# Decay rows fetched by DMA through a ring of four with a GpSimd mask, and rotation tables built first as outer products, in a hybrid SSM and attention trunk

## The chip, the cores and the metric

One Trainium2 chip, of which the kernel uses one core. The time is the device time of one execution in microseconds (us), the median over several runs. Engines are named as the profile names them: PE (TensorE; PEld is its weight load), DVE (VectorE), ACT (ScalarE), POOL (GpSimd) and SP (SyncE, which only issues DMAs here).

## The reference

The input is 2048 rows of 1024 float32 values. One layer is computed, and a final RMSNorm:

```python
h = rmsnorm(x, mix_norm_w)
proj = h @ w_in                          # columns: u | z | xbc | dt
y_s5  = s5_mixer(u, ...)                 # 16 groups of 16 channels, 64 complex states each
y_ssd = ssd_mixer(z, xbc, dt, ...)       # Mamba-2: 12 heads of 64, state 128, chunks of 128 rows
x = x + concat(y_s5, y_ssd) @ w_out
x = x + cross_attention(rmsnorm(x), rmsnorm(mem))      # 4 heads, 256 memory rows
x = x + conv_ffn(rmsnorm(x))                           # gated, causal convolution of width 3
out = rmsnorm(x)
```

Two pieces of it matter here. In `ssd_mixer` every head and chunk has a decay matrix:

```python
a_cs = cumsum(dt * a)                                  # 128 values per chunk and head
seg  = a_cs[l] - a_cs[s]
lmat = exp(where(l >= s, seg, -inf))                   # 128 x 128 per chunk and head
y_diag = (C B^T * lmat) @ (x * dt)
```

In `s5_mixer` a state rotates by a fixed complex angle with every row; the kernel works in strides of eight rows, and for that needs tables of the cosine and sine of 256 multiples of the stride's angle, for 16 groups x 64 states (1024 x 256 values each).

## The kernel before

The kernel runs its stages one after the other: the mixer (input projection, S5 preparation and SSD), the S5 stage and the output projection, the attention, the FFN. An fp32 product is made as three matmuls (`mm3`): both factors are split into a high and a low part, for a weight by ACT (L98) and DVE (L99). A loaded weight of 128x512 becomes 12 matmuls so; it is called a weight half below, as `proj` uses two of them for one projection of 512 rows.

The mixer walks over four blocks of 512 rows. A block has 22 projections, 44 weight halves. After each half `k.step()` advances two lists of generators by one yield: the foreground list has the SSD work of the block (`ssd`, in two passes `pr` of six heads), the background list has what can be done at any time: `norm1_rest` (the first norm of x's row tiles t4 to t15, whose first four, t0 to t3, are done at the start), `s5_setup`, sums of squares, preparation of the memory. This fixes the program's order; a scheduler of the tile framework then orders the instructions of each engine by its own estimates, and each engine takes its list in that order. Tiles come from pools with a fixed number of buffers (`t` has 28 of 128x512, `u` has 14 of 128x384); an instruction that wants a buffer waits until the last reader of its former content is done. `k.load` puts the weight loads on SP's queue (L111).

A norm of a row tile goes over three engines: ACT squares and sums (`ss`, L136), DVE scales (L130), POOL takes the power -0.5 (L131), DVE multiplies the row by it (L139).

`dtprep` makes `acs`, the cumulative sums of a block (128 rows x 4 chunks x 12 heads), packs a high and a low part of it into `pk`, and transposes it into `rows` (L382 to L391). `ssd` gets the decay matrices L (128 x 4 chunks x 6 heads x 128) from it: for each head one matmul that spreads the head's row over all partitions (`sel` x `rows`, L409), one that adds the mask's -1e30 (`idr` x `mask`, L410), and four exps on ACT (L412) that subtract the row's own sum (`nacs`). DVE multiplies with L at L425 and L441.

`s5_setup` computes the S5 coefficients: sines and cosines, the loads of the matrices b and c (L654), the products that go to DRAM as `cct`, `ww`, and, last, the tables. For these, `Er` and `Ei` hold the sines and cosines of the angle times powers of two, and POOL doubles a table of one column up to 256 columns, eight times for two groups each (L742 to L758), with buffers of the `t` and `u` pools, and stores it to `tabd`.

Of the kernel before, what the change touches and what calls it, by code (L numbers as in the profile page):

```python
# [173 lines left out]
class MixerIn:  # L174


    def __init__(self, k, cx, a, dram, T):
# [8 lines left out]
        x3 = flat(self.lp.tile([P, 4, 6, P], F32, tag="L", name="L").rearrange("p c h l -> p c (h l)"))  # L186
# [43 lines left out]
        sl = c([44, 12], "sl")  # L230
        V.tensor_tensor(sl, k.ident[0:44, 0:12], k.ident[0:44, 32:44], op=ALU.add)
        self.sel = []
        for i in range(3):
            s = k.t(F32R, p=44)
            V.tensor_copy(s.rearrange("p (a b) -> p a b", a=4), bcol(sl[:, 4 * i:4 * i + 4], P))
            self.sel += [s[:, q * 128:q * 128 + 128] for q in range(4)]
# [106 lines left out]
    def dtprep(self, hs, b):  # L343
# [28 lines left out]
        dt, da, acs, hr, nacs, E, cd = sm("dt"), sm("da"), sm("acs"), sm("hr", F32R), sm("nacs"), sm("E"), sm("cd")  # L372
# [9 lines left out]
        pk = self.pk[b % 2]  # L382
        V.tensor_copy(hr, acs)
        V.tensor_copy(pk[:, :, 0:12], r4(hr.bitcast(F32)))
        V.tensor_tensor(pk[:, :, 32:44], r4(acs), r4(hr.bitcast(F32)), op=ALU.subtract)
        yield
        pr = k.ps()
        for c in range(4):
            TE.transpose(pr[0:44, c * 128:c * 128 + 128], pk[:, c, :], k.ident)
        rows = k.t(F32R, p=44)  # L390
        S.activation(rows, pr[0:44, :], AF.Copy)  # L391
# [5 lines left out]
        self.dd = dict(dt=dt, rows=rows, nacs=nacs, E=E, cd=cd)  # L397
        yield

    def ssd(self, b, pr, dd, xs, Bs, Cs, zs, sqacc):  # L400
# [4 lines left out]
        L = self.lp.tile([P, 4, 6, P], F32, tag="L", name="L")  # L405
        for hh in range(6):
            h = pr * 6 + hh
            p = k.ps()
            TE.matmul(p, self.sel[h], dd["rows"], start=True, stop=False)  # L409
            TE.matmul(p, self.idr, self.mask.rearrange("p (a b) -> p a b", a=1).to_broadcast([P, 4, P]), start=False, stop=True)  # L410
# [7 lines left out]
        def stage_in(c):  # L418
            cs = slice(c * 128, c * 128 + 128)
            px = k.ps()  # L420
            for i in range(3):
                TE.transpose(px[:, i * 128:i * 128 + 128], xs[i][:, cs], k.ident)
            xdt, xdd = self.u(), self.u()
            V.tensor_tensor(r6(xdt), r6(px[:, 0:384]), v6(dd["dt"], c), op=ALU.mult)
            V.tensor_tensor(r6(xdd), r6(xdt), L[:, c, :, 127:128].to_broadcast([P, 6, 64]), op=ALU.mult)  # L425
            pB = k.ps()
            for i in range(2):
                TE.transpose(pB[:, i * 128:i * 128 + 128], Bs[i][:, cs], k.ident)
            Bt = self.u(256)
            S.activation(Bt, pB[:, 0:256], AF.Copy)  # L430
            st[c] = [xdt, xdd, Bt]

        def stage_cb(c):
            cs = slice(c * 128, c * 128 + 128)
            pc = k.ps()
            for i in range(2):
                TE.matmul(pc[:, i * 128:i * 128 + 128], Bs[i][:, cs], Cs[i][:, cs], start=True, stop=True)
            M = [self.u() for _ in range(2)]
            for i in range(2):
                m3 = M[i].rearrange("p (h l) -> p h l", h=3)  # L440
                V.tensor_tensor(m3, L[:, c, i * 3:i * 3 + 3, :], pc[:, i * 128:i * 128 + 128].rearrange("p (h l) -> p h l", h=1).to_broadcast([P, 3, P]), op=ALU.mult)  # L441
            st[c].append(M)
# [113 lines left out]
def s5_setup(k, a, d, up, NJ):  # L556
# [54 lines left out]
    yield  # L611

# [109 lines left out]
    r8 = d["r8"]  # L722
    V.tensor_tensor(r8, mag, mag, op=ALU.mult)
    V.tensor_tensor(r8, r8, r8, op=ALU.mult)
    V.tensor_tensor(r8, r8, r8, op=ALU.mult)
# [4 lines left out]
    for q in range(nst + 2):  # L730
        e, f = Er[:, q, :], Ei[:, q, :]
        V.tensor_tensor(t1, e, f, op=ALU.mult)
        V.tensor_scalar(Ei[:, q + 1, :], t1, 2.0, None, op0=ALU.mult)
        V.tensor_tensor(t1, e, e, op=ALU.mult)
        V.tensor_tensor(u1, f, f, op=ALU.mult)
        V.tensor_tensor(Er[:, q + 1, :], t1, u1, op=ALU.subtract)
    yield
    for gq in range(8):
        gs = slice(gq * 2, gq * 2 + 2)
        tc_, ts_ = k.t(), k.t()  # L740
        c3, s3 = (v.rearrange("p (g j) -> p g j", g=2) for v in (tc_, ts_))
        G.memset(c3[:, :, 0:1], 1.0)  # L742
        G.memset(s3[:, :, 0:1], 0.0)
        for q in range(nst):
            m = 1 << q
            tt = up(256).rearrange("p (g j) -> p g j", g=2)[:, :, 0:m]
            er, ei = bcol(Er[:, 3 + q, gs], m), bcol(Ei[:, 3 + q, gs], m)
            co, so, ci, si = c3[:, :, m:2 * m], s3[:, :, m:2 * m], c3[:, :, 0:m], s3[:, :, 0:m]
            G.tensor_tensor(co, ci, er, op=ALU.mult)
            G.tensor_tensor(tt, si, ei, op=ALU.mult)  # L750
            G.tensor_tensor(co, co, tt, op=ALU.subtract)
            G.tensor_tensor(so, ci, ei, op=ALU.mult)
            G.tensor_tensor(tt, si, er, op=ALU.mult)
            G.tensor_tensor(so, so, tt, op=ALU.add)
            if q >= 4:
                yield
        for h, v in ((0, c3), (1, s3)):
            G.dma_start(out=d["tab"][gs, :, h, :].rearrange("g p n -> p g n"), in_=v)  # L758
        yield
# [751 lines left out]
def trunk(tc, a, out, T):  # L1511
    with ExitStack() as cx:
# [6 lines left out]
                 tab=D([16, P, 2, NJ], "tabd"), ww=D([16, P, 256], "wwd"), cct=D([16, P, 384], "cctd"), Gt=D([4, 4, P, 512], "Gtd"), VWt=D([4, 4, P, 512], "VWtd"), p=D([T, 1024], "pd"), act=D([T // 128, P, 22, 128], "actd"),  # L1519
# [64 lines left out]
```

## Time and profile before

| | |
|---|---|
| median of three runs | 2716.18 us (2715.41 to 2720.42) |
| the profiled execution | 2718.37 us, its span 2716.6 us |
| mean granted clock of TensorE | 0.995 |
| busy: PE, DVE, ACT, POOL | 98%, 78%, 49%, 18% of the span |
| instructions | 38,961 |
| DMA | 455.6 MB, 168 GB/s on average |

The profile is of one execution. A group line has the source line, the engine, the operation and `out<-in` by the program's names, with `xcount`, busy time and the mean of one in ns; a window line has the length of the window and then, for each engine, the busy time and the number of instructions, the granted clock, the DMA share and GB/s. The tables are what POOL does between 600 and 760 us:

```profile
POOL 0000000059912110110311222211111110000000
```

This is POOL's busy share in 40 slices of 68 us, in tenths.

### The profile page before, as it was taken

The numbers are of one execution on the slowest core, as the hardware profiler recorded it, in microseconds if no ns is written. First come the engines' busy times: TensorE is split into PE (matmuls) and PEld (weight loads), VectorE is DVE, ScalarE is ACT, GpSimd is POOL, SyncE is SP. The second block draws the span as 40 slices with busy tenths as digits, with TensorE's granted clock in tenths as the row PEclk, the third lists the DMA queues.
The fourth block names the chain that finished last, engine by engine and source line by source line (L and its number), as shares of the span: only waits on it lengthen the run. The fifth ranks groups of instructions, "written<-read, shape, count | busy, mean of one in ns | idle before, by whom it ended". The sixth has DMA issues, their size and how long they took to land. (4 is left out here: it accounts for less than half of the span.)

```text
span 2716.6 us, 38961 instructions
## 1 busy us (share of the span) xinstructions
PE 2656.7 (98%) x12744; PEld 2200.2 (81%) x12744; DVE 2119.4 (78%) x4032; ACT 1322.1 (49%) x2661; POOL 484.6 (18%) x991
## 2 busy tenths in 40 slices
PE   8999999999899999999999999999999999999997
PEld 6878878788788788887888888888888888788876
DVE  8687888887777655788789788889878787677776
ACT  5565455544445413788645555345434344333233
POOL 0000000059912110110311222211111110000000
PEclk9999999999999999999999999999999999999999
DMA  6453343332378865536664333425222228887886
GB/s 196 137 160 126 94 133 108 115 100 88 109 238 270 307 235 178 175 127 237 239 220 151 113 120 122 140 83 182 86 87 85 78 63 270 273 293 239 261 268 201
DMA packets 238851, 455.57 MB, mean 168 GB/s; under 512 B 29432, under 2 KB 71416, under 8 KB 238648
## 3 DMA queue, kind: packets, MB, share of 16 engines
q1 hardware_dynamic: 182312, 341.38, 38.4%
q0 software_dynamic: 27728, 92.82, 10.5%
q10 hardware_dynamic: 28608, 18.88, 2.2%
q8 instruction: 101, 1.65, 0.3%
q14 instruction: 102, 0.84, 0.1%
HBM read 338.09 MB, written 114.29 MB: 167 GB/s over the span
## 5 line engine op out<-in xcount | busy, mean ns | idle before, releaser
L123 PE MATMUL ps<-H,W 128*128 128x512 f32 x952 | 370.7, 389 | 0.0
L125 PE MATMUL ps<-H,W 128*128 128x512 f32 x952 | 370.4, 389 | 0.0
L124 PE MATMUL ps<-H,W 128*128 128x512 f32 x952 | 370.3, 389 | 0.0
L123 PE MATMUL ps<-h,w 128*128 128x512 f32 (+1 forms) x736 | 298.6, 406 | 2.4 <-DVE h L102 1.5
L125 PE MATMUL ps<-h,w 128*128 128x512 f32 (+1 forms) x736 | 285.2, 388 | 0.0
L124 PE MATMUL ps<-h,w 128*128 128x512 f32 (+1 forms) x736 | 284.6, 387 | 0.1
L123 PE MATMUL ps<-Q,A 128*128 128x512 f32 x704 | 275.9, 392 | 1.7 <-ACT A L98 0.6
L125 PE MATMUL ps<-Q,A 128*128 128x512 f32 x704 | 274.4, 390 | 0.0
L124 PE MATMUL ps<-Q,A 128*128 128x512 f32 x704 | 274.0, 389 | 0.0
L98 ACT ACTIVATE w<-r 128x512 fp32r<-128x512 f32 x224 | 140.9, 633 | 254.2 <-PE ps L124 190.4
L98 ACT ACTIVATE W<-S 128x512 fp32r<-128x512 f32 x191 | 118.9, 630 | 282.0 <-DVE S L1337 144.8
L125 PEld LDWEIGHTS ps<-H,W 128*128 128x128 f32 x952 | 178.7, 188 | 37.1
L124 PEld LDWEIGHTS ps<-H,W 128*128 128x128 f32 x952 | 178.7, 188 | 37.0
L123 PEld LDWEIGHTS ps<-H,W 128*128 128x128 f32 x952 | 178.7, 188 | 36.9
L99 DVE TENSOR_TENSOR w<-r,w 128x512 fp32r<-128x512 f32 x224 | 158.0, 707 | 45.4 <-ACT w L98 42.3
L125 PEld LDWEIGHTS ps<-h,w 128*128 128x128 f32 x736 | 138.6, 188 | 29.6
L123 PEld LDWEIGHTS ps<-h,w 128*128 128x128 f32 x736 | 139.0, 189 | 28.2 <-DVE h L102 1.7
L124 PEld LDWEIGHTS ps<-h,w 128*128 128x128 f32 x736 | 139.2, 189 | 25.6 <-DVE h L102 1.4
L123 PEld LDWEIGHTS ps<-Q,A 128*128 128x128 f32 x704 | 132.2, 188 | 29.3 <-ACT A L98 0.9
L125 PEld LDWEIGHTS ps<-Q,A 128*128 128x128 f32 x704 | 132.2, 188 | 28.4 <-DVE A L99 0.8
L124 PEld LDWEIGHTS ps<-Q,A 128*128 128x128 f32 x704 | 132.2, 188 | 26.7
L98 ACT ACTIVATE A<-F 128x512 fp32r<-128x512 f32 (+1 forms) x146 | 89.1, 631 | 124.6 <-PE ps L124 71.2
(485 smaller groups left out, 6344.3 us busy)
## 6 DMA issues: line engine op xcount, KB each, us to landing
A<-actd SPq DMA_DIRECT2D x192, 256.0 KB, 3.9
r<-in_w_in SPq DMA_DIRECT2D x176, 256.0 KB, 2.9
R<-in_w_up SPq DMA_DIRECT2D x176, 256.0 KB, 2.9
R<-in_w_down SPq DMA_DIRECT2D x132, 256.0 KB, 4.2
actd<-U POOLq DMA_DIRECT2D x88, 256.0 KB, 3.3
A<-actd SPq DMA_DIRECT2D x96, 192.0 KB, 3.7
R<-h3Cd SPq DMA_DIRECT2D x56, 256.0 KB, 3.5
X<-in_x SPq DMA_DIRECT2D x16, 512.0 KB, 6.3
```

Source lines behind the costliest of these rows:

```text
L98: self.S.activation(hi, src, AF.Copy)
L99: self.V.tensor_tensor(lo, src, hi.bitcast(F32), op=ALU.subtract)
L123: self.TE.matmul(out, lh, rh, start=first and i == 0, stop=False)
L124: self.TE.matmul(out, lh, rl, start=False, stop=False)
L125: self.TE.matmul(out, ll, rh, start=False, stop=last and i == n - 1)
```

## The change

The decay matrices: `acs` is transposed once per block (48 rows of 128), copied to SBUF and stored to DRAM (`acsd`). `fetch_L` reads the six rows of one chunk and one pass back, broadcast to all 128 partitions (128x768), into one of four slots of `Ls`, and lets POOL write -1e30 above the diagonal with an `affine_select`. Both the DMA and the mask are on POOL's list. ACT's exps run in place in the slot. The first two chunks of a block are asked for in `dtprep`, the third at the start of `ssd`, each other one three chunks ahead of its use.

The tables: they are built right after the sines and cosines, ahead of the rest of `s5_setup`. A number j = 16 a + b: two small tables of 16 columns each for the 16 groups (`fc`, `fs` for a and for b) are doubled up in 48 products, and each of the 16 groups is then an outer product of the two by the angle sum formulas, six products of 128x256 and one store. The small tables live in the buffers in which the matrices b and c come later (tags 5b1, 5b2, 5Ca, 5Cb). The `u` and `t` pools are not used for the tables any more; `t` has 25 buffers.

```diff
@@ setup
-        mk = k.t(n=P)
-        V.tensor_scalar(mk, self.tri, 1e30, -1e30, op0=ALU.mult, op1=ALU.add)
-        self.mask = c([P, P], "mask", F32R)
-        V.tensor_copy(self.mask, mk)
-        self.idr = c([P, P], "idr", F32R)
-        V.tensor_copy(self.idr, k.ident)
...
@@ dtprep
-        pk = self.pk[b % 2]
-        V.tensor_copy(hr, acs)
-        V.tensor_copy(pk[:, :, 0:12], r4(hr.bitcast(F32)))
-        V.tensor_tensor(pk[:, :, 32:44], r4(acs), r4(hr.bitcast(F32)), op=ALU.subtract)
         yield
         pr = k.ps()
-        for c in range(4):
-            TE.transpose(pr[0:44, c * 128:c * 128 + 128], pk[:, c, :], k.ident)
-        rows = k.t(F32R, p=44)
-        S.activation(rows, pr[0:44, :], AF.Copy)
+        TE.transpose(pr[0:48, 0:P], acs, k.ident)
+        rows = self.sp.tile([48, P], F32, tag="rows", name="rows")
+        V.tensor_copy(rows, pr[0:48, 0:P])
+        k.G.dma_start(out=self.d["acs"][b].rearrange("c h l -> (c h) l"), in_=rows)
+        for c in range(2):
+            self.fetch_L(b, 0, c)
...
+    def fetch_L(self, b, pr, c):
+        L = self.Ls[:, self.nL % 4]
+        self.nL += 1
+        self.k.G.dma_start(out=L.rearrange("p h l -> p (h l)"), in_=flat(self.d["acs"][b, c:c + 1, pr * 6:pr * 6 + 6, :]).partition_broadcast(P))
+        self.k.G.affine_select(out=L, in_=L, pattern=[[0, 6], [1, P]], compare_op=ALU.is_ge, fill=-1e30, base=0, channel_multiplier=-1)
+        self.L[b, pr, c] = L
@@ ssd
-        L = self.lp.tile([P, 4, 6, P], F32, tag="L", name="L")
-        for hh in range(6):
-            h = pr * 6 + hh
-            p = k.ps()
-            TE.matmul(p, self.sel[h], dd["rows"], start=True, stop=False)
-            TE.matmul(p, self.idr, self.mask.rearrange("p (a b) -> p a b", a=1).to_broadcast([P, 4, P]), start=False, stop=True)
-            for c in range(4):
-                S.activation(L[:, c, hh, :], p[:, c * 128:c * 128 + 128], AF.Exp, bias=dd["nacs"][:, c * 12 + h:c * 12 + h + 1])
-            if hh % 2 or pr and b == self.NB - 1:
-                yield
+        Ls = {}
+        def decay(c):
+            L = Ls[c] = self.L.pop((b, pr, c))
+            for hh in range(6):
+                h = c * 12 + pr * 6 + hh
+                S.activation(L[:, hh, :], L[:, hh, :], AF.Exp, bias=dd["nacs"][:, h:h + 1])
+        if pr == 0:
+            self.fetch_L(b, 0, 2)
+        decay(0)
+        yield
...
         for c in range(4):
             stage_cb(c)
+            n = pr * 4 + c + 3
+            if n < 8:
+                self.fetch_L(b, n // 4, n % 4)
+            if c < 3:
+                decay(c + 1)
             yield
@@ s5_setup, after the sines and cosines
+    Er, Ei = (sp.tile([P, nst + 3, 16], F32, tag=n, name=n) for n in ("Er", "Ei"))
...
+    tw = sp.tile([P, 16, 8], F32, tag="tw", name="tw")
+    few = []
+    for n, q0 in (("B", 3), ("A", 7)):
+        fc, fs = (sp.tile([P, 16, 16], F32, tag="5" + x, name="f" + x) for x in (("b1", "b2") if n == "B" else ("Ca", "Cb")))
...
+        for q in range(4 if n == "B" else nst - 4):
...
+            G.tensor_tensor(co, ci, er, op=ALU.mult)
+            G.tensor_tensor(t, si, ei, op=ALU.mult)
+            G.tensor_tensor(co, co, t, op=ALU.subtract)
+            G.tensor_tensor(so, ci, ei, op=ALU.mult)
+            G.tensor_tensor(t, si, er, op=ALU.mult)
+            G.tensor_tensor(so, so, t, op=ALU.add)
+            yield
+        few.append((fc, fs))
+    (cb, sb), (ca, sa) = few
+    for g in range(16):
+        tab = sp.tile([P, 2, na, 16], F32, tag="tab", name="tab", bufs=2)
+        wk = sp.tile([P, 16, 16], F32, tag="5Ba", name="wk")[:, 0:na]
...
+        G.tensor_tensor(tab[:, 0], a_(ca), b_(cb), op=ALU.mult)
+        G.tensor_tensor(wk, a_(sa), b_(sb), op=ALU.mult)
+        G.tensor_tensor(tab[:, 0], tab[:, 0], wk, op=ALU.subtract)
+        yield
+        G.tensor_tensor(tab[:, 1], a_(sa), b_(cb), op=ALU.mult)
+        G.tensor_tensor(wk, a_(ca), b_(sb), op=ALU.mult)
+        G.tensor_tensor(tab[:, 1], tab[:, 1], wk, op=ALU.add)
+        G.dma_start(out=d["tab"][g], in_=tab.rearrange("p h a b -> p h (a b)"))
+        yield
@@ s5_setup, at its end: the doubling over 256 columns goes
-    for gq in range(8):
-        tc_, ts_ = k.t(), k.t()
...
-            tt = up(256).rearrange("p (g j) -> p g j", g=2)[:, :, 0:m]
...
-            G.tensor_tensor(co, ci, er, op=ALU.mult)
...
-        for h, v in ((0, c3), (1, s3)):
-            G.dma_start(out=d["tab"][gs, :, h, :].rearrange("g p n -> p g n"), in_=v)
@@
-            k.open(c1, 3, r=8, w=8, h=16, t=28)
+            k.open(c1, 3, r=8, w=8, h=16, t=25)
```

Three places show how the instructions stand now. The first is POOL in block 0. Before, its list has after the setup only the eighteen `ss` powers of the row tiles, and then the stores of S5 products:

```order
L220 AFFINE_SELECT tri<-tri 128x128
L229 AFFINE_SELECT last<-last 128x128
L131 TENSOR_TENSOR ss<-ss,m_71 128x1 x18
L131 TENSOR_TENSOR rs<-rs,m_71 128x4
L680 DMA cctd<-t 128x4x128
L699 MEMSET t 128x512
```

After, this is a piece around the power of tile t7 (`tab`, `wk`, `fCa`, `fb` are the new tables and their parts; `m_71` is the constant -0.5):

```order
L388 AFFINE_SELECT L<-L 128x768
L656 TENSOR_TENSOR tab<-tab,wk 128x256
L654 TENSOR_TENSOR tab<-fCa,fb_3017 128x256
L659 TENSOR_TENSOR wk<-fCa,fb_3018 128x256
L658 TENSOR_TENSOR tab<-fCb,fb_3017 128x256
L660 TENSOR_TENSOR tab<-tab,wk 128x256
L661 DMA tabd<-tab 128x512
L655 TENSOR_TENSOR wk<-fCb,fb_3018 128x256
L131 TENSOR_TENSOR ss<-ss,m_71 128x1
L656 TENSOR_TENSOR tab<-tab,wk 128x256
L659 TENSOR_TENSOR wk<-fCa,fb_3018 128x256
```

The power of t7 stands behind the small products, 21 of the large ones, and the first four fetches with their masks; those of t8 and t9 stand 38 and 28 large products further down.

The second is DVE at the same place, the scaling of t7 with the weight halves around it. Before:

```order
L99 TENSOR_TENSOR w<-r,w 128x512
L322 COPY t<-halo 128x3
L130 TENSOR_SCALAR ss<-ss 128x1
L139 TENSOR_SCALAR raw<-raw,ss 128x1024
L331 SCALAR_TENSOR_TENSOR t<-t 128x512
```

After:

```order
L99 TENSOR_TENSOR w<-r,w 128x512
L130 TENSOR_SCALAR ss<-ss 128x1
L139 TENSOR_SCALAR raw<-raw,ss 128x1024
L309 COPY halo<-t 128x3
L313 SCALAR_TENSOR_TENSOR t<-t,cw 128x512
```

The scaling stood behind the 19th weight half and stands behind the 20th; what has moved is POOL's side of the pair.

The third is SP, where the loads of the matrices b and c stand. Before they come after 14 weight loads, and their buffers are empty:

```order
L111 DMA r<-in_w_in 128x512
L654 DMA b_2997<-in_s_b 128x256
L654 DMA b_2998<-in_s_b 128x256
L654 DMA Ca<-in_s_c 128x256
L654 DMA Cb<-in_s_c 128x256
L111 DMA r<-in_w_in 128x512
```

After they come behind 37 weight loads, and go into the buffers that the small tables were read from:

```order
L705 DMA b_4924<-in_s_b 128x256
L705 DMA Cb<-in_s_c 128x256
L111 DMA r<-in_w_in 128x512
L705 DMA b_4925<-in_s_b 128x256
L705 DMA Ca<-in_s_c 128x256
L111 DMA r<-in_w_in 128x512 x3
```

So each of the four waits for POOL's last reader of that buffer, with the weight loads behind it on SP.

More of the change, by code (lines that the diff above doesn't have):

```diff
@@ L185, in __init__ @@
         cp = self.cp
-        x3 = flat(self.lp.tile([P, 4, 6, P], F32, tag="L", name="L").rearrange("p c h l -> p c (h l)"))
+        self.Ls, self.nL, self.L = self.lp.tile([P, 4, 6, P], F32, name="L"), 0, {}
+        x3 = flat(self.Ls.rearrange("p c h l -> p c (h l)"))
         self.x0 = [x3[:, 0:1024], x3[:, 1024:2048], x3[:, 2048:3072], k.raw()]
@@ L229, in __init__ @@
         G.affine_select(out=self.last, in_=self.last, pattern=[[0, P]], compare_op=ALU.is_ge, fill=0.0, base=-127, channel_multiplier=1)
[L230 to L236, printed above, removed]
         wdr = c([P, 96], "wdr")
@@ L246, in __init__ @@
         V.memset(self.halo, 0.0)
-        self.pk = [c([P, 4, 44], f"pk{i}") for i in range(2)]
-        for q in self.pk:
-            V.memset(q, 0.0)
         self.prev = [self.u() for i in range(2)]
@@ L396, in dtprep @@
         S.activation(cd, pc[:, 0:48], AF.Exp)
-        self.dd = dict(dt=dt, rows=rows, nacs=nacs, E=E, cd=cd)
+        self.dd = dict(dt=dt, nacs=nacs, E=E, cd=cd)
         yield
+    def fetch_L(self, b, pr, c):
[4 more added lines that the diff above has]
+        self.L[b, pr, c] = L
     def ssd(self, b, pr, dd, xs, Bs, Cs, zs, sqacc):
@@ L424, in stage_in @@
             V.tensor_tensor(r6(xdt), r6(px[:, 0:384]), v6(dd["dt"], c), op=ALU.mult)
-            V.tensor_tensor(r6(xdd), r6(xdt), L[:, c, :, 127:128].to_broadcast([P, 6, 64]), op=ALU.mult)
+            V.tensor_tensor(r6(xdd), r6(xdt), Ls[c][:, :, 127:128].to_broadcast([P, 6, 64]), op=ALU.mult)
             pB = k.ps()
@@ L611, in s5_setup @@
     yield
+    r8 = d["r8"]
+    V.tensor_tensor(r8, mag, mag, op=ALU.mult)
+    V.tensor_tensor(r8, r8, r8, op=ALU.mult)
+    V.tensor_tensor(r8, r8, r8, op=ALU.mult)
+    nst = NJ.bit_length() - 1
+    Er, Ei = (sp.tile([P, nst + 3, 16], F32, tag=n, name=n) for n in ("Er", "Ei"))
+    V.tensor_copy(Er[:, 0, :], cs)
+    V.tensor_copy(Ei[:, 0, :], sn)
+    for q in range(nst + 2):
+        e, f = Er[:, q, :], Ei[:, q, :]
+        V.tensor_tensor(t1, e, f, op=ALU.mult)
+        V.tensor_scalar(Ei[:, q + 1, :], t1, 2.0, None, op0=ALU.mult)
+        V.tensor_tensor(t1, e, e, op=ALU.mult)
+        V.tensor_tensor(u1, f, f, op=ALU.mult)
+        V.tensor_tensor(Er[:, q + 1, :], t1, u1, op=ALU.subtract)
+        if q % 4 == 3:
+            yield
@@ L1518, in trunk @@
                  yT=D([T // 128, P, 8, 128], "yTd"), x1=D([T, 1024], "x1d"), x2=D([T, 1024], "x2d"), h3C=D([T // 1024, 7, 4, P, 512], "h3Cd"),
-                 tab=D([16, P, 2, NJ], "tabd"), ww=D([16, P, 256], "wwd"), cct=D([16, P, 384], "cctd"), Gt=D([4, 4, P, 512], "Gtd"), VWt=D([4, 4, P, 512], "VWtd"), p=D([T, 1024], "pd"), act=D([T // 128, P, 22, 128], "actd"),
+                 tab=D([16, P, 2, NJ], "tabd"), ww=D([16, P, 256], "wwd"), cct=D([16, P, 384], "cctd"), Gt=D([4, 4, P, 512], "Gtd"), VWt=D([4, 4, P, 512], "VWtd"), p=D([T, 1024], "pd"), acs=D([T // 512, 4, 12, P], "acsd"), act=D([T // 128, P, 22, 128], "actd"),
                  rs=k.cp.tile([P, T // 128], F32, name="rs"), r8=k.cp.tile([P, 16], F32, name="r8"))
         with ExitStack() as c1:
-            k.open(c1, 3, r=8, w=8, h=16, t=28)
+            k.open(c1, 3, r=8, w=8, h=16, t=25)
             mem = Memory(k, a, d)
```

46 lines of the change are left out of this document (12 added, 34 removed).

## The prediction

> **What bounds the kernel now.** I read the engine totals first, then windows of a quiet and of a disturbed stretch, then the waits of the latter. The totals, and the two windows (length, then busy time and instructions of PE, PEld, DVE, ACT and POOL, granted clock, DMA share, GB/s):
>
> ```profile
> PE 2656.7 (98%) x12744; PEld 2200.2 (81%) x12744; DVE 2119.4 (78%) x4032; ACT 1322.1 (49%) x2661; POOL 484.6 (18%) x991
> 100.00:200.00 100.00, 99.35 (x511) 80.22 (x511) 74.56 (x167) 58.98 (x128) 3.19 (x5) 1.00 0.48 148
> 600.00:760.00 160.00, 146.21 (x798) 123.96 (x797) 119.81 (x233) 74.03 (x162) 125.06 (x313) 0.96 0.32 102
> ```
>
> PE is the bound: 98% busy over the span, 99.35 us of 100 in block 0. A matmul that goes is therefore time won at its start-to-start distance, as long as DVE and ACT, which prepare PE's weights, keep ahead. The exception is 600 to 760 us, where POOL, almost idle elsewhere, is busy for 125 us building the rotation tables. PE idles there for 13.8 us at a mean clock of 0.96, another 6.4 us worth: 20 us together. The largest waits of that stretch are these (engine, what waits, for what: total us, times, longest):
>
> ```profile
> DVE u L452 <- POOL t L754: 6.5, 2, 3.9
> DVE u L424 <- POOL t L754: 6.0, 3, 3.5
> DVE u L441 <- POOL t L754: 3.5, 2, 2.2
> ```
>
> DVE waits for the `u` buffers that POOL's table code also takes from. That coupling goes with the change.
>
> **The products removed.** One stretch of PE's timeline (start, duration, instruction) and the groups by form (count, busy, mean ns):
>
> ```profile
> 94.54 0.49 PE L409 MATMUL ps<-t 44*128 44x512 f32 x1
> 94.96 0.49 PE L410 MATMUL ps<-mask,idr 128*128 128x512 f32 x1
> 95.39 0.49 PE L409 MATMUL ps<-t 44*128 44x512 f32 x1
> L410 PE MATMUL ps<-mask,idr 128*128 128x512 f32 x48 | 23.9, 497 | 0.0
> L409 PE MATMUL ps<-t 44*128 44x512 f32 x48 | 23.8, 495 | 0.0
> L389 PE MATMUL ps<-ident,pk 128*44 128x128 f32 x16 | 2.4, 272 | 0.0
> ```
>
> They start 0.42 us apart (94.54, 94.96, 95.39), so 96 of them hold PE for 40.3 us; 12 of the 16 transposes go too, at an estimated 0.1 us of pitch each (a quarter of the 512-wide row). Of the 96, 12 belong to the first half of block 0 and lie in front of the delay worked out next, which swallows them. The other 84 and 9 transposes are worth 84 × 0.42 + 0.9 = **-36.1 us**, all on the path. With them go the packing of `pk` and `hr` on DVE, one ACT copy a block and the setup of `sel`, `mask` and `idr`: none of it was the last thing PE waited for; I cost it at 0, covered by the weights in flight, at most -2.
>
> **The tables moved to the front.** This is the largest term. POOL's stream now has, in block 0: the sums of squares `ss` (L131) of the first x tiles, 48 small products, then 16 groups of six 128x256 products and a DMA, with the first four decay fetches, their masks, and the `ss` of tiles t7, t8 and t9 between them. An engine takes its instructions in order, which the 25.88 us of the first row below show: a POOL DMA waited for ACT with ready products behind it. Durations from the old tables and nearby rows:
>
> ```profile
> 543.02 0.77 POOL L680 DMA_DIRECT2D wwd<-t  x1 [25.88 <-ACT t L719]
> 643.77 0.73 POOL L749 TENSOR_TENSOR t<-t,Er 128x16 f32<-128x16 f32 x1
> 652.97 0.61 POOL L749 TENSOR_TENSOR t<-t,Er 128x256 f32<-128x256 f32 x1
> L749 POOL TENSOR_TENSOR t<-t,Er 128x256 f32<-128x256 f32 x8 | 5.3, 667 | 0.0
> L750 POOL TENSOR_TENSOR u<-t,Ei 128x256 f32<-128x256 f32 x8 | 6.3, 791 | 0.0
> L751 POOL TENSOR_TENSOR t<-t,u 128x256 f32<-128x256 f32 x8 | 7.1, 892 | 0.6
> L752 POOL TENSOR_TENSOR t<-t,Ei 128x256 f32<-128x256 f32 x8 | 4.9, 612 | 0.0
> L753 POOL TENSOR_TENSOR u<-t,Er 128x256 f32<-128x256 f32 x8 | 6.2, 778 | 0.6
> L754 POOL TENSOR_TENSOR t<-t,u 128x256 f32<-128x256 f32 x8 | 6.9, 864 | 0.2
> 637.20 0.79 POOL L758 DMA_DIRECT2D tabd<-t  x1
> 639.07 0.73 POOL L758 DMA_DIRECT2D tabd<-t  x1 [0.22 <-POOL t L743]
> L1460 POOL DMA_DIRECT2D F<-in_final_norm_w x1 | 0.6, 558 | 0.0
> L699 POOL MEMSET t<- 128x512 f32 x4 | 2.2, 549 | 0.0
> L220 POOL TENSOR_SCALAR_AFFINE_SELECT tri<-tri 128x128 f32<-128x128 f32 x1 | 0.3, 293 | 0.0
> t<-cctd POOLq DMA_DIRECT2D x16, 192.0 KB, 5.0
> ```
>
> From 643.77 to 652.97 the old code ran the four doublings of 16, 32, 64 and 128 elements, 24 products: 9.2 us. The new code runs two such builds, 18.4 us. A group of the new tables is the sum of the six means, 4.60, and 0.73 for the DMA: 5.3 us (bounds: six at 0.61 and 0.73, 4.4; six at 0.892 and 0.79, 6.1). The mask over 128x768 has no row: the 128x128 one took 0.293, six of those would be 1.76, and a fill of 512 elements scaled to 768 gives 0.82; I take 1.3, the middle, as both neighbours are far. Four fetches and the store of the rows are five issues at 0.56, the four masks 5.2, and the first mask waits for its rows to land, 5.0 less three issues: 3.3. Together 11.3 us. Where POOL stands against DVE, in the trace of before:
>
> ```profile
> 45.55 0.70 DVE L99 TENSOR_TENSOR w<-r,w 128x512 fp32r<-128x512 f32 x1
> 68.94 0.55 POOL L131 TENSOR_TENSOR ss<-ss,m 128x1 f32<-128x1 f32 x1 [14.34 <-DVE ss L130]
> 69.52 0.75 DVE L139 TENSOR_SCALAR raw<-raw,ss 128x1024 f32<-128x1024 f32 x1 [0.66 <-POOL ss L131]
> 86.01 0.76 DVE L139 TENSOR_SCALAR raw<-raw,ss 128x1024 f32<-128x1024 f32 x1 [0.73 <-POOL ss L131]
> 100.63 0.75 DVE L139 TENSOR_SCALAR raw<-raw,ss 128x1024 f32<-128x1024 f32 x1 [0.73 <-POOL ss L131]
> 0.00:117.80 117.80, 89.22 (x368) 67.76 (x369) 23.26 (x34) 21.24 (x34) 1.00 0.54 173
> r<-in_w_in SPq DMA_DIRECT2D x176, 256.0 KB, 2.9
> ```
>
> The powers that the tables start from are DVE work that in the new order is done by about 45.5 us (the first row is its neighbour there). The small products then end near 64.5. DVE comes to the scaling of t7 at 69.52, as before. Ahead of that `ss` POOL has 21 products and three stores, 3.5 groups, and the fetches with their masks, 18.6 + 11.3 = 29.9 us from 64.5: near 94. t8 follows 6.3 groups later at 128, t9 4.7 groups after that at 154. Behind each waiting scaling stand DVE's weight halves (L99), hence PE. ACT's first exps wait for the first mask, near 80 us, inside the same delay.
>
> Then comes a fourth wait. The loads of the S5 matrices go into the buffers of the small tables, so SP holds them, and the weight loads behind them, until POOL's last read: 64.5 + 15.8 × 5.3 + 11.3 + three `ss` at 0.6 = 161.3 us. Issue 0.5, landing 2.9 (the last row), two DVE products 1.3 and the half itself 0.7 bring PE to the 32nd weight half at 166.7 us. Before, 31 halves are 372 matmuls; the window row on the weight tile counts 368 by 117.8, so PE began the 32nd near 118.7. The delay is **+48.0 us** (34 to 63 by the group bounds and the mask's).
>
> **The rest.** In 600 to 760 us the 20 us of loss should fall to what the quiet window has, 1; the S5 products that used to run earlier now run nearer to it, so I take **-15** (-19 to -5). PE restarts after four stalls. One such restart is in the trace (PE alone: window, busy, clock):
>
> ```profile
> 690.00:692.00 2.00, 0.00 (x0) 0.75 0.37 130
> 692.00:694.00 2.00, 1.02 (x5) 0.50 0.21 63
> 694.00:696.00 2.00, 2.00 (x10) 0.50 0.18 69
> 696.00:698.00 2.00, 2.00 (x6) 0.54 0.41 131
> ```
>
> 5.0 us of work ran at half clock, so up to 2.5 us were lost; I take 2 each, **+8** (0 to 10). The Trainium skill, "TensorE: Matmul & The Clock Gate", Part 1 (The HAM clock gate), says that the clock is halved after about 3.4 us idle and is given back after about 3.4 us of work; that would be 1.7 each, 6.8 in all, and the sum 1.2 lower. The trace's dip is longer than that rule gives.
>
> In blocks 1 to 3 and the second half of block 0 POOL issues 28 more fetches and masks, 28 × 1.86 = 52 us spread over some 600 us, each asked for three chunks before its use. A mask that waits for its landing blocks what is behind it on POOL, which there are stores of S5 matrices with time to spare; the exps behind it on ACT are the risk. **+3** (0 to 10). The exps themselves are as many as before.
>
> Sum: -36.1 + 48.0 - 15 + 8 + 3 = +7.9 us. The profiled execution took 2718.4 us, 2.2 above the median of the runs, 2716.2: 2726 for a profile, **2724** against the median.
>
> **Rivals.**
> First, the tables are hidden and DVE is never held. For that POOL has to reach the `ss` of t7 by 69 us, 24 after it may start. The small products alone are 18 of that, so the order would have to run otherwise on the chip than it stands. Then only -41 and -15 remain: **2660**. Against it: the in-order row above. Chance 0.08; this is the case on the other side.
> Second, POOL is cheaper than its old rows, since those ran beside a busy DVE: at 4.4 us a group and 0.82 a mask the delay is 34 to 36, and with the whole relief of 19 the sum is -10 to -17: **2700 to 2708**, to 2712 with less relief. It decides from about 4.6 us a group. For it: 0.61 for a product in the row at 652.97. Chance 0.17.
> Third, the groups run at the dear rows throughout, 6.1 us, as DVE is as busy in block 0 as in the old window: +12.6, and a late fetch or two adds up to 10: **2737 to 2750**. The 0.892 row speaks for it. The Trainium skill's "GPSIMD Engine Reference", section 1 (Specifications), says that GpSimd shares its SBUF interfaces with VectorE and contends with two-input instructions there. By that rule each product of a group would be dear, +12.6; the trace agrees only for three of six. Chance 0.13.
> The forecast itself has 0.62; its own range is 2712 to 2738.
>
> **Range and chances.** A measurement of this kernel tells about 0.2% from no change, 2710.8 to 2721.6. Of the forecast's 0.62, 0.15 lies within that and 0.47 above; of the second rival 0.12 is below it and 0.05 within; the first is faster, the third slower. So faster 0.20, same 0.20, slower 0.60. The range leaves out the first rival and the far tails: 2700 to 2752.
>
> **What would show it.** Right: DVE's scalings of t7, t8 and t9 waiting for POOL's `ss` by some 24, 17 and 11 us; the 32nd weight half near 167; PE's count lower by 96 products and 12 transposes; no wait of DVE on POOL in 600 to 760 us. Wrong: `ss` rows at 69 and 86 us as before (first rival); a group of tables under 4.6 us (second) or over 5.8 (third); the S5 loads landing before 150 us; ACT waiting for masks for more than 10 us after block 0; a granted clock of 1.00 through the stalls.

## The result and the profile after

The changed kernel takes 2738.3 us (median, 2734.8 to 2741.6), the kernel before 2718.3 us beside it: a ratio of 1.0074, with a 95% interval of 1.0056 to 1.0092. It is 20 us slower. The forecast was 2724 within 2700 to 2752; its sign holds, and so does its main mechanism, POOL's chain in block 0; its size is 14 us short. The profiled execution took 2741.6 us, 23 more than that of before.

First the engine totals and POOL's 40 slices of the page after, then three windows of after, and last the first of these for the kernel before (length, then busy time and count of PE, PEld, DVE, ACT and POOL, granted clock, DMA share, GB/s):

```profile
PE 2625.9 (96%) x12636; PEld 2187.3 (80%) x12636; DVE 2136.0 (78%) x4015; ACT 1324.6 (48%) x2657; POOL 482.3 (18%) x807
POOL 3840101101103110110311222212111111000000
```

```profile
60.00:180.00 120.00, 67.81 (x291) 54.58 (x290) 70.77 (x100) 38.59 (x85) 99.08 (x135) 0.76 0.40 130
600.00:760.00 160.00, 145.87 (x809) 125.60 (x808) 133.79 (x286) 84.58 (x183) 22.88 (x31) 0.95 0.37 118
720.00:750.00 30.00, 17.03 (x85) 14.76 (x82) 21.34 (x46) 12.98 (x23) 3.69 (x6) 0.72 0.39 119
```

```profile
60.00:180.00 120.00, 120.00 (x593) 97.31 (x593) 92.88 (x198) 72.81 (x148) 3.74 (x6) 1.00 0.47 147
```

PE lost its 108 instructions and 31 us of work. But in block 0, where it was busy for 120 of 120 us, it now works for 68, at a mean clock of 0.76: POOL's block of table work has moved from slices 9 to 11 to slices 1 to 3, and PE stands still beside it. The window of 600 to 760 us, from which the tables are gone (POOL 125 us before, 23 now), idles as long as it did, 14.1 us against 13.8; the loss has a new place, 720 to 750 us.

This is POOL's way through block 0, a selection of its timeline (start, duration):

```profile
44.48 0.24 POOL L640 TENSOR_TENSOR tw<-fb,Ei 128x16 f32<-128x16 f32 x1 [6.22 <-DVE Xr L675]
63.44 1.07 POOL L654 TENSOR_TENSOR tab<-fCa,fb 128x256 f32<-128x256 f32 x1
82.25 0.87 POOL L388 TENSOR_SCALAR_AFFINE_SELECT L<-L 128x768 f32<-128x768 f32 x1 [2.65 <-DMA L<-acsd]
93.91 0.57 POOL L131 TENSOR_TENSOR ss<-ss,m 128x1 f32<-128x1 f32 x1
130.39 0.56 POOL L131 TENSOR_TENSOR ss<-ss,m 128x1 f32<-128x1 f32 x1
158.11 0.56 POOL L131 TENSOR_TENSOR ss<-ss,m 128x1 f32<-128x1 f32 x1
166.16 0.74 POOL L660 TENSOR_TENSOR tab<-tab,wk 128x256 f32<-128x256 f32 x1
167.77 0.55 POOL L387 DMA_DIRECT2D L<-acsd  x1
173.22 0.87 POOL L388 TENSOR_SCALAR_AFFINE_SELECT L<-L 128x768 f32<-128x768 f32 x1 [4.90 <-DMA L<-acsd]
```

The small products, the first large one, the first mask, the powers of t7, t8 and t9, the last large product, the fifth fetch and its mask. And these are the PE instructions at which its five long gaps end (the gap in brackets):

```profile
84.42 0.79 PE L123 MATMUL ps<-h,w 128*128 128x512 f32 x1 [10.52 <-ACT w L98]
95.79 1.11 PE L148 MATMUL ps<-ident,raw 128*128 128x128 f32 x4 [5.92 <-DVE raw L139]
132.34 1.09 PE L148 MATMUL ps<-ident,raw 128*128 128x128 f32 x4 [19.11 <-DVE raw L139]
160.99 0.79 PE L430 MATMUL ps<-t 128*128 128x128 f32 x2 [16.14 <-DVE t L316]
740.61 1.09 PE L768 MATMUL ps<-ident,t 128*128 128x128 f32 x4 [12.22 <-DVE t L727]
```

The first four sum to 51.7 us. The first ends with ACT, which stood at its first exps until the first mask; the other three end with DVE, behind the scalings of t7, t8 and t9. The fifth, at the end of the mixer, was in no term of the sum.

To follow the delay, the same matmul is found in both profiled runs by its number among the 2208 that read the mixer's weight tile (`ps<-h,w`):

| matmul number (its start before) | 372 (121 us) | 440 (142) | 880 (290) | 1400 (463) | 2050 (679) | 2110 (705) | 2200 (831) |
|---|---|---|---|---|---|---|---|
| after, us later than before | +58 | +60 | +51 | +35 | +29 | +23 | +21 |

### The profile page after: what moved, and what is told of

Read it like the earlier page. It is cut to its first block, busy times and chain, and to the rows that moved or that the text cites. A ratio compares the mean times of both kernels' runs of the same rounds, so it can differ in the third digit from the quotient of the medians.

```text
span 2739.9 us, 38565 instructions
## 1 busy us (share of the span) xinstructions
PE 2625.9 (96%) x12636; PEld 2187.3 (80%) x12636; DVE 2136.0 (78%) x4015; ACT 1324.6 (48%) x2657; POOL 482.3 (18%) x807
## 5 line engine op out<-in xcount | busy, mean ns | idle before, releaser
L123 PE MATMUL ps<-h,w 128*128 128x512 f32 (+1 forms) x736 | 301.8, 410 | 13.4 <-ACT w L98 10.5
L125 PE MATMUL ps<-h,w 128*128 128x512 f32 (+1 forms) x736 | 288.9, 392 | 0.5 <-DVE w L99 0.5
L124 PE MATMUL ps<-h,w 128*128 128x512 f32 (+1 forms) x736 | 287.6, 391 | 0.7 <-DVE h L102 0.7
L123 PEld LDWEIGHTS ps<-h,w 128*128 128x128 f32 x736 | 140.8, 191 | 38.8 <-ACT w L98 10.9
```

The source lines that it names most:

```text
L123: self.TE.matmul(out, lh, rh, start=first and i == 0, stop=False)
L124: self.TE.matmul(out, lh, rl, start=False, stop=False)
L125: self.TE.matmul(out, ll, rh, start=False, stop=last and i == n - 1)
```

## The experiments

All ratios are to the kernel before, run on the same chip. The first five split the change.

**decay_alone.** The table code of before put back at its old place, the rest as changed:

```diff
-    for g in range(16):
-        tab = sp.tile([P, 2, na, 16], F32, tag="tab", name="tab", bufs=2)
...
+    for gq in range(8):
+        gs = slice(gq * 2, gq * 2 + 2)
+        tc_, ts_ = k.t(), k.t()
...
```

> The decay part of the change alone: rows by DMA, ring of four, mask on POOL; the tables are doubled up at their old place at the end of the S5 setup, with the old buffers (t pool 25). Theory A (the loss of the change is the table chain on POOL in block 0, the decay part is a plain gain): the 96 products and 12 transposes are worth 41, the old loss of 20 between 600 and 760 us stays, some masks wait behind table products there (up to 5): 2675 to 2690, no PE gap over 2 us before 600 us. Theory B (the ring is to blame, masks come late for ACT's exps and PE waits as it does at 74 to 84 us of the changed kernel): 2705 or more, with gaps of PE in every block.

Measured 2711.2 us, ratio 0.9977 (0.9967 to 0.9987). Neither: no gap of PE over 2.2 us from 8 to 580 us, nearly as A has it, but only 7 us won. The window of the tables is where it is lost, PE busy for 131.1 us of 160 in place of 146.2:

```profile
600.00:760.00 160.00, 131.07 (x723) 114.95 (x722) 112.37 (x214) 59.39 (x125) 124.39 (x306) 0.88 0.31 99
```

Two waits of that window (total us, times, longest) say how, ACT's exps for masks and PE for the products of L:

```profile
ACT L L403 <- POOL L L388: 24.4, 4, 7.9
PE ps L457 <- DVE u L434: 13.7, 5, 8.2
```

**tables_alone.** The new table code on the kernel before.

```diff
+    for g in range(16):
+        tab = sp.tile([P, 2, na, 16], F32, tag="tab", name="tab", bufs=2)
...
-    for gq in range(8):
-        gs = slice(gq * 2, gq * 2 + 2)
...
-            k.open(c1, 3, r=8, w=8, h=16, t=28)
+            k.open(c1, 3, r=8, w=8, h=16, t=25)
```

> The tables part alone: outer products right after the sines and cosines, on the kernel before with its decay products on PE (t pool 25, for space). Theory A: POOL's chain is the same without the four fetches and masks (11 us), so the scalings of t8 and t9 still wait; delay after block 0 about 40 with the clock, minus the 19 of the old table window, plus the 17 of the new gap near 730 us: 2750 to 2765. Theory B (fetches and masks hold the chain): under 2730.

Measured 2772.2 us, 1.0200 (1.0184 to 1.0215): A, and 7 us more. The delay after block 0 is 53 us without a single fetch, in two gaps of 18.4 and 23.2 us that end with scalings (L139). The tables alone stop block 0.

**tables_last.** The whole change, the table code moved behind the S5 products.

```diff
-    for g in range(16):
-        tab = sp.tile([P, 2, na, 16], F32, tag="tab", name="tab", bufs=2)
...
             put(d["ww"][gs, :, w * 128:w * 128 + 128], Ws)
             yield
...
+    for g in range(16):
+        tab = sp.tile([P, 2, na, 16], F32, tag="tab", name="tab", bufs=2)
...
```

> The whole change, but the outer-product tables are built at the old place, behind the S5 products. Theory A: nothing holds block 0 and nothing pushes the S5 products to the end; 41 from the products and about 19 from the old table window, since the new tables use no t or u buffers: 2655 to 2668. Theory B (POOL beside the fetches is the problem wherever the tables stand): masks wait behind table products in blocks 2 and 3, ACT and PE with them: 2690 or more.

Measured 2705.3 us, 0.9957 (0.9944 to 0.9970). Block 0 is free, A's half; but at 488 to 619 us PE has seven gaps of 1 to 8.2 us, 27 us in all, where POOL issues the 16 table stores in a row from 513 to 599 us, and the next block's first fetch comes at 601.5. B's half.

**before_no_tables and decay_no_tables.** The products of the tables are left out of the kernel before and of decay_alone.

```diff
-        for q in range(nst):
-            m = 1 << q
...
-            G.tensor_tensor(so, so, tt, op=ALU.add)
+        G.memset(tc_, 1.0)
+        G.memset(ts_, 0.0)
+        for q in range(4):
+            yield
```

> The kernel before without the table products: POOL fills each table with ones and stores it, so the S5 output is another one; everything else as before. It prices what the tables cost where they stood. Theory (the loss of 20 in 600 to 760 us is the tables): 2697 to 2702.

> decay_alone (rows by DMA, ring, mask on POOL) without the table products, which are replaced by fills with ones as in before_no_tables. Theory C (decay_alone fell short by 31 us because masks and fetches stand behind table products on POOL, and table products behind masks): without the products the full price of the 108 PE instructions shows, 41 below before_no_tables: 2655 to 2662. Theory D (with the products gone PE is no longer what sets the mixer's end, DVE and ACT are, or the ring itself is late in every block): 2675 or more, with PE gaps or a lower rate in all blocks.

Measured 2697.9 us, 0.9912 (0.9897 to 0.9926), and 2664.1 us, 0.9792 (0.9777 to 0.9806). The first is in its range; the second lies between C and D, 2 us above C. Without table products the decay part is worth 33 to 34 us, and PE runs on through the window, 154.7 us with 1055 matmuls at full clock:

```profile
600.00:760.00 160.00, 154.73 (x1055) 142.20 (x1054) 129.72 (x278) 82.42 (x175) 23.80 (x41) 1.00 0.55 178
```

With these the change splits into six cells, each a ratio to the kernel before. Two more things differ between them: the early tables are outer products and those at the old place are doublings, and the `t` pool has 28 buffers in the first two cells of the first row, 25 in the others. For the first, tables_last, with outer products at the old place, has 0.9957 against 0.9977, some 5 us; no run prices the second.

| | no table products | tables at the old place | tables early |
|---|---|---|---|
| decay on PE | 0.9912 | 1 | 1.0200 |
| decay by DMA | 0.9792 | 0.9977 | 1.0074 |

Across the first row the tables cost 24 us at the old place and 78 early; across the second 50 and 77. The decay part gains 33 us with no tables, 34 with early ones, and 6 where the old tables share POOL's list with its fetches. The change as made is the sum: 24 won, 33 won, 77 lost, 20 slower.

**power_on_dve and power_on_dve_own_buffers.** The first takes POOL out of the norm, the second also gives the small tables buffers of their own.

```diff
-        self.rstd(ss, ss, 1.0 / 1024, 1e-6)
+        V.tensor_scalar(ss, ss, 1.0 / 1024, 1e-6, op0=ALU.mult, op1=ALU.add)
+        V.tensor_scalar(y, ss, -0.5, 1.5, op0=ALU.mult, op1=ALU.add)
+        for _ in range(2):
+            V.tensor_tensor(t, y, y, op=ALU.mult)
+            V.scalar_tensor_tensor(t, t, -0.5, ss, op0=ALU.mult, op1=ALU.mult)
+            V.scalar_tensor_tensor(y, t, 1.5, y, op0=ALU.add, op1=ALU.mult)
@@ power_on_dve_own_buffers as well
-        fc, fs = (sp.tile([P, 16, 16], F32, tag="5" + x, name="f" + x) for x in (("b1", "b2") if n == "B" else ("Ca", "Cb")))
+        fc, fs = (sp.tile([P, 16, 16], F32, tag="6" + x, name="f" + x) for x in (("b1", "b2") if n == "B" else ("Ca", "Cb")))
```

> The changed kernel with the power -0.5 of the row norms done on DVE by two Newton steps (eight small instructions instead of one and a POOL product), so that no scaling waits for POOL. The S5 loads still go into the small tables' buffers. Theory A (as in the prediction: the S5 loads alone would hold DVE until POOL's last table read): the scalings no longer wait, but PE runs dry after the 31st weight half until about 170 us: 2725 to 2738. Theory B (the held scalings are the whole loss, the S5 loads cost only the 5 us that DVE waited there): 2690 to 2705, with PE gaps in block 0 of the first masks alone (10 us) and about 5 at the S5 loads.

> power_on_dve, and the small tables in buffers of their own (t pool 24, for space), so that the S5 loads wait for nothing. If the PE gap of 22 us at 146 to 168 us of power_on_dve is the wait for those loads, it goes, and with it 22 to 27: 2712 to 2720. If the late masks alone hold PE there, nothing changes: 2735 or more.

Measured 2741.1 us, 1.0084 (1.0069 to 1.0099), and 2745.0 us, 1.0086 (1.0069 to 1.0103): nothing won by either; both lie above 2735, as the second expectation has it for late masks alone. The waits of 140 to 175 us of the first, then those of 140 to 180 us of the second, and POOL at the end of its tables in the second:

```profile
ACT L L411 <- POOL L L396: 33.7, 1, 33.7
DVE b L714 <- DMA b<-in_s_b: 24.0, 1, 24.0
```

```profile
ACT L L411 <- POOL L L396: 38.6, 1, 38.6
PE ps L423 <- DVE u L453: 29.2, 1, 29.2
```

```profile
169.17 0.59 POOL L669 DMA_DIRECT2D tabd<-tab  x1 [0.30 <-POOL tab L668]
169.76 0.54 POOL L395 DMA_DIRECT2D L<-acsd  x1
173.88 0.87 POOL L396 TENSOR_SCALAR_AFFINE_SELECT L<-L 128x768 f32<-128x768 f32 x1 [3.58 <-DMA L<-acsd]
```

With the norm off POOL, DVE waits for the S5 loads for 24.0 us and ACT for the fifth mask for 33.7. With the loads free as well, only ACT's wait for the fifth mask is left, 38.6 us, because the fifth fetch stands behind the last table product. Three chains waited for the same end; undoing two left the third. And DVE is late by itself, too: in power_on_dve a gap of PE of 10.4 us still ends with a norm's product on DVE at 121 us, and DVE was busy for 25.6 of the 26 us before it (95 to 121).

**nothing_waits_on_pool.** The third is undone too.

```diff
-        self.k.G.dma_start(out=L.rearrange("p h l -> p (h l)"), in_=flat(self.d["acs"][b, c:c + 1, pr * 6:pr * 6 + 6, :]).partition_broadcast(P))
-        self.k.G.affine_select(out=L, in_=L, pattern=[[0, 6], [1, P]], compare_op=ALU.is_ge, fill=-1e30, base=0, channel_multiplier=-1)
+        self.k.nc.sync.dma_start(out=L.rearrange("p h l -> p (h l)"), in_=flat(self.d["acs"][b, c:c + 1, pr * 6:pr * 6 + 6, :]).partition_broadcast(P))
+        self.k.V.tensor_tensor(L, L, self.mask.rearrange("p (a b) -> p a b", a=1).to_broadcast([P, 6, P]), op=ALU.add)
```

> power_on_dve_own_buffers with the decay rows stored and fetched on SP's queue and the mask added by DVE (128x768, 32 times), so that POOL has only the early tables in block 0 and nobody there waits for it. Theory F (in block 0 three chains waited for the end of POOL's table work at once: the norm's powers, the S5 loads, and the fifth fetch, so that undoing one or two gave nothing): all stalls of 60 to 180 us go, the delay of 57 with them; what stays is the late S5 gap (17) and DVE's extra 25 to 30 us of masks, which its idle time covers in part: 2680 to 2700. Rival G (POOL's products slow DVE and PE down by sharing the memory, whoever waits): 2715 or more, with DVE's weight halves (0.7 us) longer in 60 to 165 us.

Measured 2712.4 us, 0.9974 (0.9963 to 0.9986): 27 us better than the changed kernel by the ratios, but not F's 2680 to 2700, and 3 us under G's 2715. The delay after block 0 (matmul 500) is 32 us, with nobody waiting for POOL. What PE waits for there is DVE, and DVE's instructions are slower. Its groups of 60 to 165 us by form, in before, in after and in this kernel (count, busy, mean ns), and the window of 60 to 180 us of this kernel, with DVE busy for 115.7 of 120 us:

```profile
L99 DVE TENSOR_TENSOR w<-r,w 128x512 fp32r<-128x512 f32 x29 | 19.9, 687 | 5.4 <-ACT w L98 4.0 <-PE ps L437 1.1 <-PE ps L148 0.2
L441 DVE TENSOR_TENSOR u<-L,ps 128x384 f32<-128x384 f32 x8 | 4.1, 548 | 0.0
L324 DVE COPY halo<-t 128x3 f32<-128x3 f32 x11 | 1.8, 162 | 0.0
```

```profile
L99 DVE TENSOR_TENSOR w<-r,w 128x512 fp32r<-128x512 f32 x17 | 17.6, 1035 | 10.5 <-ACT w L98 10.5
L434 DVE TENSOR_TENSOR u<-L,ps 128x384 f32<-128x384 f32 x2 | 1.0, 540 | 0.0
L309 DVE COPY halo<-t 128x3 f32<-128x3 f32 x7 | 4.2, 597 | 0.0
```

```profile
L99 DVE TENSOR_TENSOR w<-r,w 128x512 fp32r<-128x512 f32 x22 | 25.9, 1177 | 0.0
L428 DVE TENSOR_TENSOR u<-u,L 128x384 f32<-128x384 f32 x3 | 3.3, 1105 | 0.0
L444 DVE TENSOR_TENSOR u<-L,ps 128x384 f32<-128x384 f32 x6 | 3.1, 542 | 0.0
```

```profile
60.00:180.00 120.00, 96.87 (x455) 79.48 (x453) 115.74 (x181) 56.35 (x124) 101.36 (x128) 0.91 0.48 157
```

On average a weight half takes 687 ns beside an idle POOL and 1177 beside the new table products. (Beside the old ones, at 600 to 750 us of the kernel before, it took 775.) So what G named is there as well. But not all of the 32 us is G's. From 60 us to matmul 500 DVE is busy for 128.9 us, in the kernel before for 78.5. By the means of each form some 29 of these 50 us are the same instructions running slower; the rest is work that this kernel adds, eight masks (8.7 us) and the Newton steps (about 14, themselves slowed). How PE's delay divides between the two, the run does not separate.

**tables_spread and tables_on_dve.** The tables half a group at a time between the S5 products, with results in the t pool; first on POOL, then on DVE with stores on ACT's queue.

```diff
+    tg = tables()
+    for i, _ in enumerate(products()):
+        if i < 8 or i % 2 == 0:
+            next(tg, None)
+        yield
...
-        tab = sp.tile([P, 2, na, 16], F32, tag="tab", name="tab", bufs=2)
+        tab = k.t().rearrange("p (h a b) -> p h a b", h=2, b=16)
@@ tables_on_dve as well
-        G.tensor_tensor(tab[:, 0], a_(ca), b_(cb), op=ALU.mult)
+        V.tensor_tensor(tab[:, 0], a_(ca), b_(cb), op=ALU.mult)
...
```

> The whole change with the outer-product tables built half a group at a time between the S5 products, with their result in buffers of the t pool, which the scheduler cannot hoist past the products; nothing of them in block 0. Theory C: a mask or a fetch finds at most a few table products ahead of it, so nearly the full 41 and 19 are won: 2660 to 2675. Theory D: 2690 or more.

> tables_spread with the table products on DVE in place of POOL and their stores on ACT's queue: POOL keeps fetches, masks and the S5 stores. Theory C (the loss of tables_spread is order on POOL's list: table products wait behind S5 stores that wait for ACT, fetches wait behind table products): most of the 50 between decay_no_tables and tables_spread comes back, less 35 to 40 us of DVE work that DVE has idle time for: 2670 to 2690. Rival H (any engine that does the tables in 280 to 540 us costs as much, as DVE is 85% busy there): 2705 or more.

Measured 2714.3 us, 0.9972 (0.9962 to 0.9983), and 2693.1 us, 0.9902 (0.9887 to 0.9917). Spread on POOL misses theory C by 40 us; D is right. POOL's list is held by its own stores there, with table products behind them:

```profile
385.76 0.95 POOL L724 TENSOR_TENSOR wk<-fSb,fb 128x256 f32<-128x256 f32 x1
404.00 0.80 POOL L696 DMA_DIRECT2D wwd<-t  x1 [17.28 <-ACT t L772]
404.82 0.64 POOL L723 TENSOR_TENSOR t<-fSa,fb 128x256 f32<-128x256 f32 x1
```

On DVE 19 of the 49 us above decay_no_tables come back, by the ratios. The second lies 3 us above theory C's range and 12 below H's. What is still missing goes with a fuller DVE: the windows of 300 to 600 us of tables_spread, tables_on_dve and decay_no_tables, in this order:

```profile
300.00:600.00 300.00, 271.97 (x1348) 223.56 (x1347) 259.49 (x523) 134.22 (x271) 119.60 (x155) 0.94 0.41 130
```

```profile
300.00:600.00 300.00, 280.08 (x1456) 228.84 (x1455) 276.21 (x671) 143.37 (x293) 38.54 (x51) 0.98 0.43 137
```

```profile
300.00:600.00 300.00, 296.10 (x1569) 248.02 (x1568) 263.87 (x609) 164.10 (x340) 49.05 (x68) 1.00 0.44 138
```

DVE is busy for 276 of 300 us, and PE for 280 where it could be for 296. So H is partly right in kind: DVE takes 33 us more (2141 against 2109 over the span), and it looks as if not all of it fits into the time that DVE had idle; no run shows this apart. This is still the fastest kernel here that builds the tables, 27 us below before.

**fewer_yields and no_table_yields.** Both go for the gap at 728 us, the late S5 products.

```diff
@@ fewer_yields
-            for _ in range(4):
-                yield
+            yield
             p = k.ps()
             for i in range(4):
                 TE.transpose(p[:, i * 128:i * 128 + 128], WT[:, i * 128:i * 128 + 128], k.ident)
@@ no_table_yields
             G.tensor_tensor(so, so, t, op=ALU.add)
-            yield
...
         G.tensor_tensor(tab[:, 0], tab[:, 0], wk, op=ALU.subtract)
-        yield
...
         G.dma_start(out=d["tab"][g], in_=tab.rearrange("p h a b -> p h (a b)"))
-        yield
```

> The changed kernel, with one yield in place of four ahead of each transpose of the S5 products, so that these products, which the tables' 40 yields pushed back, are through well before the mixer ends. Theory E (the PE gap of 12 us at 728 us and the slow clock behind it are the pushed-back S5 products, and ate the gain of the emptied table window): the gap goes, 14 to 17 won: 2720 to 2725. Rival: the gap only moves into the blocks (the products come denser there): 2733 or more.

> The changed kernel with the yields between the table products taken out and nothing else: POOL's list in block 0 stands as in the changed kernel, but the S5 products come 40 yields sooner, at the place that they had before. Theory E (the tables' yields pushed the S5 products to the end of the mixer, and the PE gap at 728 us with the slow clock behind it is what ate the gain of the emptied table window): the stalls of 74 to 161 us stay, the gap of 12 us at 728 us goes, 14 to 18 won against the changed kernel: 2720 to 2725. Rival: the emptied window gave nothing in any case (the S5 products cost the same wherever they stand, or block 3 has another bound): 2733 or more.

fewer_yields: 2757.3 us, 1.0130 (1.0113 to 1.0147), worse than the rival. The gap at 728 us is gone, but PE now stands for 5.4, 5.4 and 7.1 us at 523 to 581 us, at the transposes whose distance to their input the yields had kept. That edit took away two things at once, so its time alone told nothing on theory E. no_table_yields: 2733.3 us, 1.0055 (1.0034 to 1.0076), not told apart from 1.0074. Here the gap is gone, and no such gaps come in its place; the windows of 680 to 760 us of the changed kernel and of this one:

```profile
680.00:760.00 80.00, 65.87 (x387) 58.11 (x386) 64.05 (x137) 37.00 (x75) 10.12 (x13) 0.89 0.35 112
```

```profile
680.00:760.00 80.00, 79.43 (x471) 69.91 (x469) 65.36 (x142) 42.00 (x89) 5.73 (x8) 1.00 0.33 105
```

PE has 13.6 us more work in that window, and the run ends hardly sooner. The delay, by the method of the table above, says where the gain goes:

| matmul number | 440 | 1400 | 2050 | 2200 |
|---|---|---|---|---|
| changed kernel, us later than before | +60 | +35 | +29 | +21 |
| no_table_yields | +61 | +52 | +44 | +17 |
| fewer_yields | +61 | +38 | +62 | +36 |
| decay_no_tables | +2 | -17 | -28 | -55 |

From matmul 2050 to 2200, the emptied window, the changed kernel takes back 9 us, the two runs without the late gap 26 and 27, as much as decay_no_tables. So the late S5 products did eat the gain of the window, as theory E has it. But from 440 to 2050 the changed kernel takes back 31 us and decay_no_tables 29, no_table_yields only 17: what the early tables do not cost at the end, they cost in blocks 1 to 3. For the time the rival is right: removing the gap does not bring the gain.

## Why the prediction was right, and where it was short

**The products, -36.1.** Right. With no tables around, the decay part is worth 33 to 34 us over the whole kernel, and from matmul 440 to the mixer's last, 35 us (decay_no_tables against before_no_tables). The 5 us of the first half of block 0 are not seen even there: a gap of 1.8 us at 101 us and a short dip of the clock (0.83 from 100 to 110 us) stand in their place.

**POOL's chain, +48.** Right in mechanism and nearly in size. The small products started at 44.5 (45.5 expected), the large ones at 63.4 (64.5), the powers of t7, t8 and t9 came at 93.9, 130.4 and 158.1 (94, 128, 154), the last product at 166.2 (161.3). Twelve groups from 98.4 to 167.8 us, with two powers between, took 5.7 us each, against 5.3. The mask was 0.87 us, nearer the scaled fill than the middle taken. The delay with the clock was 60 against 56. Three details were off. The sum goes by the S5 loads as the last wait; they were issued at 164.7 to 166.5 us, when PE had come out of its last gap, and the own-buffers run shows that freeing them wins nothing while the fifth fetch waits for the same end. That fetch, which stands behind the whole table work too, was not in the sum at all. So the size came near with some luck: it was worked out from one chain, others held PE, and it fits because all of them end with POOL's tables. And a part of the delay is DVE's slower pace, which the third rival priced on POOL's side alone. Behind the wait for the first mask, and with its own slower instructions, DVE came to the scaling of t7 at 87.5 us, not at 69.5, and so it waited for the three powers for 6.9, 13.2 and 11.2 us instead of 24, 17 and 11.

**The clock, +8.** Right: 60 less 51.7 of gaps leaves 8. The matmuls after the 9.1 us gap of nothing_waits_on_pool show one such restart:

```profile
88.94 0.63 PE L124 MATMUL ps<-h,w 128*128 128x512 f32 x1
89.37 0.63 PE L125 MATMUL ps<-h,w 128*128 128x512 f32 x1
90.19 0.40 PE L124 MATMUL ps<-h,w 128*128 128x512 f32 x1
90.42 0.40 PE L125 MATMUL ps<-h,w 128*128 128x512 f32 x1
```

From 85.0 to 89.8 us matmuls start 0.43 us apart, then 0.23: some 10 of them lost 0.2 each, 2 us. The Trainium skill, "TensorE: Matmul & The Clock Gate", Part 1 (The HAM clock gate), gives about 3.4 us of work until the clock is back; here it was 4.8.

**The emptied table window, -15.** This is the step that failed. before_no_tables shows that 24 us were there to win. The changed kernel won 4: its delay is 21 at the mixer's end, where 60 - 35 leaves 25. The prediction said only that S5 products "now run nearer to it". The tables' 40 yields pushed those to 742 us, and a gap of 12.2 us with a slow clock (0.72 at 720 to 750 us) ended the mixer. Against decay_no_tables, which has the same decay part and no tables, the early tables cost 58 us by matmul 440, nothing more up to 2050, and 18 from there to 2200. In tables_alone against before_no_tables that last stretch costs 20. So in these two kernels what the early tables cost beyond block 0 is paid around the late S5 products. Moving the products back did not win it: no_table_yields saves the 18 us there and loses 12 us against decay_no_tables before, from 440 to 2050, where PE's idle time is 10.9 us against 5.1 and its clock 0.99 against 1.00. (The profiled run of it was 5 us longer than its median, so a part of the 12 may be that run's own.) What causes these losses stays open. Late masks do not explain them: from 190 to 560 us ACT waits for masks for 29.7 us in no_table_yields, and for 28.3 in the changed kernel, which loses nothing there.

**Masks, +3.** Not more than that. ACT waited for masks after block 0 for 41.7 us in all (180 to 760 us, 17 waits of at most 5.7 us), and the prediction had called more than 10 a sign of being wrong. The waits are as long in decay_no_tables (37.7 us from 120 to 720 us), and there 35 of the 36 us come. So ACT's waits were a poor sign: hardly any of them reached PE. Another 3 us, from a delay of 21 to one of 23, came behind the mixer, and were in no term.

**The rivals.** The first, DVE never held, fell with the powers at 94, 130 and 158 us. The second needed groups below 4.6 us; single ones took 4.9 where DVE stood waiting. The third, dear groups throughout, has the time in its range, 2737 to 2750, but not for its reason: groups of 5.7 us in place of 5.3 account for about 5 us. It is half right on the groups, as single products took 0.61 us while DVE waited and 1.07 while it worked. The Trainium skill, "GPSIMD Engine Reference", section 1 (Specifications), says that the SBUF interfaces are shared with VectorE, with contention for DVE instructions of two SBUF inputs or in a two-port mode. The rows agree, and in both directions: halves with two SBUF inputs went from 687 to 1035 ns and in nothing_waits_on_pool to 1177, `u<-u,L` there from 552 to 1105, while products that read one input from PSUM stayed (`u<-L,ps`, 548, 540 and 542). The section names no size; beside the new tables single products took up to 1.75 times as long on POOL, and the halves 1.5 to 1.7 times as long on average on DVE.

## What to carry to other kernels

When work moves to an engine that looks idle, list all that stands behind it on that engine's list, and who waits for each: here the norm's powers, the S5 loads and the fifth fetch all waited for one table, and undoing one or two of the three won nothing. Price a part alone, with the other part removed altogether and not only at its old place: the decay part was worth 33 us with no tables, 6 with them at the old place and 34 with them early. And when work goes to the front of a list of yields, ask what it pushes to the back: here the S5 products, to where nothing covered them. A cheap-looking helper engine is not free for its neighbour either, so look at the durations of the bound engine's suppliers while it runs, not only at their waits.

## What the runs showed of the hardware

POOL's 128x256 products and DVE's 128x512 ones slow each other: 0.61 to 1.07 us on POOL, 0.69 to 1.04 or 1.18 on DVE beside the outer products of the tables, 0.69 to 0.78 beside the old doublings. Of the forms shown, small DVE copies suffer most: a 128x3 copy went from 162 to 597 ns, about the length of one POOL product. So an engine that nobody waits for can still hold back another one's instructions, the short ones above all.
